# A two-layer trunk on one core: output projection of two heads by seven products of halves, the seven products in another order, part of layer 1's modulation later

## The chip, the cores and the metric

One Trainium2 chip, one core of it. The time is the device time of one execution in microseconds (us). The kernel before took 725.39 us as the median of 3 runs (724.83 to 725.51). The profile that is read here is of one execution of that kernel.

## What is computed

The trunk has two layers over 512 positions of width 1024: layer 0 is a retention mixer with 4 heads (keys 256 wide, values 512 wide), layer 1 a forgetting attention with 16 heads. Each layer is an adaLN-modulated RMS norm, the mixer, and a gated residual add. The part that matters here is layer 0:

```python
shift, scale, gate = jnp.split(c_act @ mod_w[i] + mod_b[i], 3, axis=-1)
h = _rms_norm(x, norm_g[i]) * (1.0 + scale[:, None, :]) + shift[:, None, :]
# _retention(h): w_in gives q, k (rope), values v and a gate path g
q, k, v, g = jnp.split(h @ w_in, [RET_DK, 2 * RET_DK, 2 * RET_DK + RET_DV], axis=-1)
...                                   # chunkwise retention of 4 heads -> o
o = _layer_norm(_from_chunks(o)).reshape(b, s, RET_DV)
y = (o * jax.nn.silu(g)) @ w_out      # w_out is 2048 x 1024: the output projection
x = x + gate[:, None, :] * y          # then layer 1's norm, and layer 1
```

## The kernel before, in words

**Numbers and matmuls.** Every f32 factor of a product is split into a high part (a cast to fp32r on ACT, the tile `wh` for weights) and a low part (the difference, on DVE, `wl`). A product is three matmuls, high by high, high by low and low by high (`mm3`), each 128 x 128 by 128 x 512.

**Order.** Nothing runs in the order of the source. Each instruction is recorded as a task with a priority, and a list scheduler (`Sched.order`) with its own costs lays out one fixed order for each engine. Buffers come from pools by kind: `KINDS` says how many of a kind there may be, and the eight PSUM banks (pool Z) are shared by the kinds `p`, `r`, `s` and `a`. All instructions are issued at one line (L442, in the changed kernel L448), so views of the profile are read by tile names. Each engine takes its instructions strictly in that order, so that an instruction which waits holds everything behind it on its engine. `merge` interleaves a main stretch of work with a side stretch.

**Heads of layer 0.** `head(h)` projects q and k, and then values and gates by `values_gates`: the 512 x 1024 by 1024 x 1024 product is cut into 2 x 2 halves and made by seven products of halves in place of eight (a scheme of Strassen's kind). One product is 24 matmuls of 128 x 512 into two banks. Its weight operand is a block of the weights, a sum of two blocks that DVE adds (`raw<-raw,raw`), or a sum that an accumulating DMA on POOL's queue adds in place (`plus`). Its other operand is a quarter of the transposed input (tiles `act`) or a sum of quarters (tiles `sf`). Banks that hold a partial result and are still needed are copied to `u` on ACT. While head h is projected, the retention of head h-1 runs beside it.

In all heads the products come in this order: first block by quarter (0,0) into banks x; second block by quarter (0,1) into y, then the values of the upper half are put out; sum 1 into v; sum 4 on top of v; sum 2 on top of x, then the gates of the upper half; sum 3 on top of x, then the gates of the lower half (`put_g(1, ...)`, which DVE makes as `big<-u,p`); last quarter (1,1) on top of x. The last product writes the banks that `put_g(1)` reads.

**Output projection.** The gated heads are transposed on the PE (`make_goT`, tiles `go`), the weights are loaded, multiplied by the residual gate on DVE (`raw<-raw,gate`, two of 128 x 512 for a loaded block) and split. `out_a(0)` and `out_a(1)` do heads 0 to 2 for the two halves of the columns into eight accumulators `a`, `out_last` does head 3 tile by tile; `merge(out_a(0), tail3(), ...)` puts head 3's retention beside the first. Then `norm_a(t)` adds the accumulator to x (`x<-a,x`), squares, and rescales (`xn<-x,t`), and `norm_b(t)` transposes (`r<-ident,xn`), modulates and splits into layer 1's input `big`. The first projection of layer 1 is `p<-wh,big`.

**Modulation.** A chunk of shift, scale or gate is a sum over 8 rows of weights on DVE (`macc<-raw,csilu,macc`). Twelve chunks of it (`extra`) are put between the heads' weights.

Of the kernel before, what the change touches and what calls it, by code (L numbers as in the profile page):

```python
# [28 lines left out]
R0, R1, R2 = 0.45, 0.5, 0.84  # L29
# [16 lines left out]
ROPE_AT = 24  # L46

GO = -6.0
# [473 lines left out]
def trunk(tc, x, c, positions, mod_w, mod_b, norm_g, ret_w_in, ret_w_out, fox_w_in, fox_b_f,  # L522
# [6 lines left out]
    with ExitStack() as es:  # L529
# [276 lines left out]
        extra = [its[i:i + 2] for its in extra for i in (0, 2)]  # L806

# [241 lines left out]
        def values_gates(h):  # L1049
# [3 lines left out]
            vc, gc = vcol(h), gcol(h)  # L1053
# [9 lines left out]
            def whole(n):  # L1063
                return [R(("vg", h, n), i) for i in range(2)]

            def plus(raw, col, lo):
                with s.at(SUMS):
                    for i in range(2):
                        G.dma_start(raw[i].rearrange("p (k n) -> p k n", k=2, n=512), rows2(wi0, col, lo + i),
                                    accum_op=ALU.add)  # L1070
                return heads(raw)

# [20 lines left out]
            put_v, put_g = values_out(h), gates_out(h)  # L1093
            x, y, v = [], [], []
            def sum2(raw, other):

                def f(i):
                    V.tensor_tensor(out=raw[i], in0=raw[i], in1=other()[i], op=ALU.add)
                    return heads(raw)(i)
                return f  # L1100

            kept = {}

            def block(n):
                if n not in kept:
                    kept[n] = whole(n)
                return kept[n]
# [563 lines left out]
```

## Time and profile before

| what | value |
|---|---|
| median of 3 runs | 725.39 us (724.83 to 725.51) |
| profiled execution, its own time | 727.05 us |
| span of the profiled execution | 725.3 us |
| PE matmul busy | 706.3 us, 97% of the span |
| DVE busy | 586.7 us, 81% |
| ACT busy | 394.1 us, 54% |
| POOL busy | 118.6 us, 16% |
| mean granted TensorE clock | 0.992 |

The span is the time from the first to the last instruction in the trace; 1.75 us of the execution lie around it. "Busy" of PE comes from matmul records whose ends are modelled and overlap their successors, so the spacing of starts is what a matmul costs. The engine PEld is the loading of the PE's stationary operand.

### The profile page before, as it was taken

What the parts mean: (1) busy time and instruction counts of PE and PEld (TensorE: products, weight loads), DVE (VectorE), ACT (ScalarE), POOL (GpSimd) and SP (SyncE); (2) the same over time, 40 slices, a digit from 0 to 9 for tenths busy, and PEclk for the clock granted to TensorE, in tenths of its full rate; (3) what the DMA queues carried; (4) which work ended last, traced back from release to release, by engine and by line L of the source; (5) the groups of instructions that cost most, each with busy time, mean ns of one, the idle gap of its engine ahead of it and who ended that gap; (6) DMA issues with size and microseconds to landing.
All of it is one profiled execution on the core that took longest, in us unless ns stands there. A gap on an engine that the chain in (4) does not pass through costs nothing.

```text
span 725.3 us, 10079 instructions
## 1 busy us (share of the span) xinstructions
PE 706.3 (97%) x3386; PEld 579.3 (80%) x3386; DVE 586.7 (81%) x1273; ACT 394.1 (54%) x733; POOL 118.6 (16%) x167
## 2 busy tenths in 40 slices
PE   7999999999998999999999999999999999999995
PEld 6777888888887888888888887788887788888884
DVE  5899999989995899899561878887696977789925
ACT  6557574644354426564140553556676577789513
POOL 1001100110100010100000100054343355531011
PEclk9999999999999999999999999999999999999998
DMA  8993773895657755726254317395646565645202
GB/s 288 350 306 81 180 224 105 217 246 173 161 145 174 232 136 151 193 87 204 89 172 145 118 43 249 133 246 142 168 113 155 124 161 138 172 112 186 87 14 103
DMA packets 78547, 118.26 MB, mean 163 GB/s; under 512 B 6952, under 2 KB 39840, under 8 KB 78496
## 3 DMA queue, kind: packets, MB, share of 16 engines
q1 hardware_dynamic: 66176, 98.71, 42.4%
q0 software_dynamic: 12320, 18.91, 14.4%
q8 instruction: 27, 0.44, 0.2%
q14 instruction: 24, 0.20, 0.1%
HBM read 109.16 MB, written 4.25 MB: 156 GB/s over the span
## 4 chain that ended last, share of the span: by engine, by line
PE 82%; DMA 7%; DVE 5%; ACT 3%; issue 2%; POOL 1%; SPq 0%; DVEq 0%; ACTq 0%; POOLq 0%
PE p L442 46%; PE a L442 18%; PE r L442 16%; DMA raw<-in_mod_w 3%; DMA tg<-in_positions 1%; PE s L442 1%; DMA ck<-in_k_mask 1%; DVE macc L442 1%; DVE t L442 1%; POOL lg L442 1%; ACT st L442 1%; DVE st L442 1%; ACT lg L442 1%; ACT wh L442 1%; DMA x<-in_x 1%
## 5 line engine op out<-in xcount | busy, mean ns | idle before, releaser
L442 ACT CAST wh<-raw 128x1024 fp32r<-128x1024 f32 x120 | 124.8, 1052 | 81.4 <-PE p L442 40.5
L442 DVE TENSOR_TENSOR wl<-raw,wh 128x1024 fp32r<-128x1024 f32 x120 | 146.0, 1222 | 26.7 <-ACT wh L442 23.6
L442 PE MATMUL p<-wh,big 128*128 128x512 f32 x384 | 135.7, 402 | 0.0
L442 PEld LDWEIGHTS p<-wh,big 128*128 128x128 f32 x384 | 71.8, 189 | 13.1
L442 PE MATMUL p<-wh,sf 128*128 128x512 f32 x256 | 80.0, 390 | 0.0
L442 PE MATMUL p<-wl,big 128*128 128x512 f32 x192 | 76.5, 398 | 0.0
L442 PE MATMUL p<-wh,act 128*128 128x512 f32 x192 | 64.1, 396 | 1.9 <-DVE big L442 1.9
L442 POOL DMA_DIRECT2D raw<-in_ret_w_in x16 | 19.4, 1240 | 269.6 <-DVE raw L442 88.4
L442 DVE SCALAR_TENSOR_TENSOR macc<-raw,csilu,macc 128x512 f32<-128x512 f32 x80 | 59.8, 747 | 3.5 <-DMA raw<-in_mod_w 2.7
L442 PE MATMUL a<-wh,go 128*128 128x512 f32 x192 | 61.7, 392 | 0.0
L442 PEld LDWEIGHTS p<-wh,sf 128*128 128x128 f32 x256 | 48.0, 188 | 10.8 <-ACT u L442 0.7
L442 POOL TENSOR_SCALAR lg<-lg,t 128x512 f32<-128x512 f32 (+1 forms) x64 | 42.6, 714 | 83.0 <-DVE t L442 68.9
L442 PE MATMUL p<-act,wh 128*128 128x512 f32 x160 | 53.1, 393 | 0.0
L442 PE MATMUL p<-wl,sf 128*128 128x512 f32 x128 | 50.0, 391 | 0.0
L442 PE MATMUL p<-big,wh 128*128 128x512 f32 x128 | 46.3, 419 | 0.0
L442 PEld LDWEIGHTS p<-wh,act 128*128 128x128 f32 x192 | 36.0, 188 | 9.1 <-issue 2.3
L442 PEld LDWEIGHTS a<-wh,go 128*128 128x128 f32 x192 | 36.0, 188 | 7.0
L442 PEld LDWEIGHTS p<-wl,big 128*128 128x128 f32 x192 | 36.2, 189 | 6.2
L442 ACT ACTIVATE lg<-lg,t 128x512 f32<-128x512 f32 (+1 forms) x64 | 35.9, 563 | 9.2 <-DVE t L442 8.7
L442 PE MATMUL r<-act,sh 128*128 128x512 f32 x120 | 40.6, 391 | 0.0
L442 PE MATMUL p<-wl,act 128*128 128x512 f32 x96 | 38.3, 399 | 1.1 <-DVE wl L442 1.1
L442 PE MATMUL a<-wl,go 128*128 128x512 f32 x96 | 37.7, 393 | 0.0
(184 smaller groups left out, 1514.5 us busy)
## 6 DMA issues: line engine op xcount, KB each, us to landing
raw<-in_ret_w_in SPq DMA_DIRECT2D x48, 512.0 KB, 6.1
raw<-in_mod_w SPq DMA_DIRECT2D x64, 256.0 KB, 6.7
raw<-in_fox_w_in SPq DMA_DIRECT2D x32, 512.0 KB, 4.2
raw<-in_ret_w_in POOLq DMA_DIRECT2D x16, 512.0 KB, 8.9
raw<-in_mod_w SPq DMA_DIRECT2D x16, 512.0 KB, 4.6
raw<-in_ret_w_out SPq DMA_DIRECT2D x16, 512.0 KB, 4.3
ck<-cum_dram SPq DMA_DIRECT2D x16, 448.0 KB, 4.4
x<-in_x SPq DMA_DIRECT2D x16, 256.0 KB, 5.3
```

Of the source, the lines that this page charges most:

```text
L442: getattr(eng, op)(*[real(v) for v in args], **{k: real(v) for k, v in kw.items()})
```

## The change

Four things are altered.

1. The output projection of heads 0 and 1 (rows 0 to 1023 of `w_out`) goes by the same seven products of halves: `values_gates` becomes a general `halves`, `make_halves` makes the quarters and sums of the transposed gated heads, and `put_o` puts the results out. Heads 2 and 3 stay with three matmuls per product of tiles into the accumulators `a`.
2. The residual gate is multiplied on the results (`residual`: one multiply `oa<-..,gate`, one add into x) and no longer on the weights. Results of heads 0 and 1 are added into x as they come; those of heads 2 and 3 in `norm_a`. The loads of x stand ahead of the output projection.
3. The seven products come in another order. In all heads sum 2 stands before sum 4, and the last product's accumulating DMA is issued right after sum 2. In heads 1 to 3 (`LAST`) the second product (quarter (0,1) into y) is made late, between sum 3 and the last product.
4. Of the twelve extra chunks of modulation four (`LATE_SS`, layer 1's shift and scale of columns 4 to 7) come between the output weights and not between the heads' weights. Head 0's rope is started at step 32 and not 24; the pool takes six `sx` and four `oa`.

```diff
-R0, R1, R2 = 0.45, 0.5, 0.84
+R0, R1, R2, R3 = 0.45, 0.5, 0.84, 0.35
...
 
-ROPE_AT = 24
-
-GO = -6.0
+ROPE_AT = 32
+
+LATE_SS = 4
+
+GO = (-20.0, -15.0, -10.0, -5.0)
+
+LATER = 4.0
+
+LAST = (1, 2, 3)
...
-            return WItem(wo0[:, 2 * i:2 * i + 2, nh * 512:nh * 512 + 512], 2, 512, (0, nh * 512), place)
+            return WItem(wo0[:, 2 * i:2 * i + 2, nh * 512:nh * 512 + 512], 2, 512, place=place)
...
-            for n in range(4):
+            for i, n in enumerate((0, 2, 3, 1) if h in LAST else range(4)):
                 add(("vg", h, n), its[2 * n:2 * n + 2])
-                if h > 0 and n % 2:
+                if h > 0 and i % 2:
                     spread()
+        its = w_halves(wo0, 0, 512, 0, 2)
+        for n in range(4):
+            add(("oh", n), its[2 * n:2 * n + 2])
         while extra:
             spread()
+        spread2()
         for nh in range(2):
-            add(("o", nh), [w_o(i, nh) for i in range(6)])
+            add(("o", nh), [w_o(i, nh) for i in (4, 5)])
+            spread2()
         for i in (6, 7):
             for nh in range(2):
                 add(("o", nh, i), [w_o(i, nh, lambda k: [act() for _ in range(k)])])
+                spread2()
...
+        def halves(key, src, cols, lows, quarter, sums, put, late=False):
...
             first = block(0)
+
+            def second():
+                yield from product(y, lambda: quarter(0, 1), heads(block(1)), True)
+                put(0, 0, y, u1, ALU.add)
+
             yield from product(x, lambda: quarter(0, 0), heads(first), True)
             u1 = keep(x)
-            yield from product(y, lambda: quarter(0, 1), heads(block(1)), True)
-            put_v(0, y, u1)
-            yield from product(v, lambda: forms[1], sum2(first, lambda: block(2)), True)
-            third = plus(block(2), gc, 2)
+            if not late:
+                yield from second()
+            yield from product(v, lambda: sums[1], sum2(first, 2), True)
+            third = plus(block(2), c1, lo)
             u5 = keep(v)
-            yield from product(v, lambda: forms[4], heads(block(3)), False)
-            yield from product(x, lambda: forms[2], sum2(first, lambda: block(3)), False)
+            yield from product(x, lambda: sums[2], sum2(first, 3), False)
+            fourth = plus(first, c0, lo)
             u2 = keep(x)
-            put_g(0, v, u2)
-            yield from product(x, lambda: forms[3], third, False)
-            put_g(1, u5, x)
-            yield from product(x, lambda: quarter(1, 1), plus(first, vc, 2), False)
-            put_v(1, x, None)
+            yield from product(v, lambda: sums[4], heads(block(3)), False)
+            put(0, 1, v, u2, ALU.subtract)
+            yield from product(x, lambda: sums[3], third, False)
+            put(1, 1, u5, x, ALU.subtract)
+            if late:
+                yield from second()
+            yield from product(x, lambda: quarter(1, 1), fourth, False)
+            put(1, 0, x, None, None)
...
+        def values_gates(h):
+            put_v, put_g = values_out(h), gates_out(h)
+
+            def put(i, j, a, b, op):
+                if j:
+                    put_g(i, a, b)
+                else:
+                    put_v(i, a, b)
+            yield from halves(("vg", h), wi0, (vcol(h), gcol(h)), (0, 2), quarter, forms, put, h in LAST)
...
-            mm3(ps, goT[kt][0][:, ts], goT[kt][1][:, ts], wh, wl, kt == 0, kt == 15)
-
-        with s.at(GO):
-            for h in range(2):
-                run(make_goT(h))
...
-        def out_a(nh):
-            for i in range(6):
-                wh, wl = W(("o", nh), i)
+            mm3(ps, goT[kt][0][:, ts], goT[kt][1][:, ts], wh, wl, kt == 8, kt == 15)
+
+        def gated(t, nh):
+            return gate_t[:, nh * 512:nh * 512 + 512]
+
...
+        def residual(t, nh, y, out=None):
+
+            out = s.buf("oa") if out is None else out
+            V.tensor_tensor(out=out, in0=y, in1=gated(t, nh), op=ALU.mult)
+            V.tensor_tensor(out=x1s[t][nh], in0=out, in1=x1s[t][nh], op=ALU.add)
...
+        def make_halves(b):
+
+            lo, hi = slice(0, 256), slice(256, 512)
+            pss = []
...
+                ps = pr_()
...
+                    last_t[:] = [T.transpose(ps[:, t * P:(t + 1) * P], go[h][t][:, b * P:(b + 1) * P], ident)]
+                yield 0.45
+                pss.append(ps)
...
+            f0, s13, s24 = s.buf("sx"), s.buf("sx"), s.buf("sx")
+            A.copy(f0, pss[0])
+            for key, src, c in (((0, 0), pss[0], lo), ((0, 1), pss[1], lo), ((1, 1), pss[1], hi)):
+                n = 256 if key == (0, 1) else 0
+                if not n:
+                    h, l = s.buf("go", 512, F32R), s.buf("go", 512, F32R)
+                hc, lc = h[:, n:n + 256], l[:, n:n + 256]
+                split(src[:, c], hc, lc)
+                quarters[key][b] = (hc, lc)
+            V.tensor_tensor(out=s13[:, lo], in0=f0[:, hi], in1=pss[1][:, hi], op=ALU.subtract)
+            V.tensor_tensor(out=s13[:, hi], in0=f0[:, lo], in1=f0[:, hi], op=ALU.subtract)
+            V.tensor_tensor(out=s24[:, lo], in0=s13[:, lo], in1=f0[:, lo], op=ALU.subtract)
+            V.tensor_tensor(out=s24[:, hi], in0=pss[1][:, lo], in1=s24[:, lo], op=ALU.add)
+            for src, (n1, n2) in ((s13, (1, 3)), (s24, (2, 4))):
+                h, l = s.buf("go", 512, F32R), s.buf("go", 512, F32R)
+                split(src, h, l)
+                sums[n1][b] = (h[:, lo], l[:, lo])
+                sums[n2][b] = (h[:, hi], l[:, hi])
+
+        def put_o(i, j, a, b, op):
+            with s.at(LATER):
+                for tl in range(2):
+                    if b is None:
+                        residual(2 * i + tl, j, a[tl])
+                    else:
+                        y = s.buf("oa")
...
+                        V.tensor_tensor(out=y, in0=a[tl], in1=b[tl], op=op)
+                        residual(2 * i + tl, j, y, y)
...
+        for b in range(4):
+            with s.at(GO[b]):
+                run(make_halves(b))
...
-        merge(out_a(0), tail3(), 1.0, B0, s)
+        load_x()
+        merge(halves(("oh",), wo0, (0, 512), (0, 2), lambda i, j: quarters[i, j], sums, put_o), tail3(), R3, B0, s)
...
             for nh in range(2):
-                V.tensor_tensor(out=x1[nh], in0=acc[nh, t], in1=x1[nh], op=ALU.add)
+                residual(t, nh, acc[nh, t], xns[t][nh])
...
+        acc = {}
+        with s.after(*last_t):
+            for nh in range(2):
+                for i in range(2):
+                    wh, wl = W(("o", nh), i)
+                    for t in range(NT):
+                        if i == 0:
+                            acc[nh, t] = s.buf("a")
+                        for k in range(2):
+                            out_mm(acc[nh, t], 8 + 2 * i + k, t, wh[k], wl[k])
+        wlast = {(nh, i): W(("o", nh, i)) for i in (6, 7) for nh in range(2)}
```

On the PE, at the end of head 2's seven products: `p_440` and `p_444` are the banks x, `sf4` are sums of quarters (product 6, sum 3), `act` are plain quarters. Before, product 7 follows product 6 on the same banks:

```order
L442 MATMUL p_444_2000<-wh_490_2193,sf4_144_701 128x512
L442 MATMUL p_444_2000<-wh_490_2193,sf4_164_776 128x512
L442 MATMUL p_444_2000<-wl_491_2200,sf4_164_776 128x512
L442 MATMUL p_444_2000<-wh_490_2193,sf4_167_786 128x512
L442 MATMUL p_440_1987<-wh_498_2237,act_99_513 128x512 [waits DVE_49,Activation_49]
L442 MATMUL p_440_1987<-wl_499_2249,act_99_513 128x512
L442 MATMUL p_440_1987<-wh_498_2237,act_104_532 128x512
L442 MATMUL p_440_1987<-wh_498_2237,act_106_537 128x512
L442 MATMUL p_440_1987<-wl_499_2249,act_106_537 128x512
L442 MATMUL p_440_1987<-wh_498_2237,act_108_546 128x512
L442 MATMUL p_444_2000<-wh_498_2237,act_99_513 128x512 [waits DVE_49]
L442 MATMUL p_444_2000<-wl_499_2249,act_99_513 128x512
```

In the changed kernel the banks x are `p_440` and `p_442`. Behind product 6 on the PE comes first the late second product, into `p_487` and `p_490`:

```order
L448 MATMUL p_442_1996<-wh_470_2129,sf4_144_701 128x512
L448 MATMUL p_442_1996<-wh_470_2129,sf4_164_776 128x512
L448 MATMUL p_442_1996<-wl_473_2143,sf4_164_776 128x512
L448 MATMUL p_442_1996<-wh_470_2129,sf4_167_786 128x512
L448 MATMUL p_487_2220<-wh_475_2152,act_99_513 128x512 [waits Activation_49]
L448 MATMUL p_487_2220<-wl_478_2166,act_99_513 128x512 [waits DVE_49]
L448 MATMUL p_487_2220<-wh_475_2152,act_104_532 128x512
L448 MATMUL p_487_2220<-wh_475_2152,act_106_537 128x512
```

and behind its last rows product 7, on the banks x:

```order
L448 MATMUL p_490_2232<-wh_480_2175,act_123_615 128x512
L448 MATMUL p_490_2232<-wh_480_2175,act_124_618 128x512
L448 MATMUL p_490_2232<-wl_482_2186,act_124_618 128x512
L448 MATMUL p_490_2232<-wh_480_2175,act_128_633 128x512
L448 MATMUL p_440_1985<-wh_483_2196,act_99_513 128x512 [waits DVE_49,Activation_49]
L448 MATMUL p_440_1985<-wl_489_2226,act_99_513 128x512 [waits DVE_49]
L448 MATMUL p_440_1985<-wh_483_2196,act_104_532 128x512
L448 MATMUL p_440_1985<-wh_483_2196,act_106_537 128x512
L448 MATMUL p_440_1985<-wl_489_2226,act_106_537 128x512
L448 MATMUL p_440_1985<-wh_483_2196,act_108_546 128x512
L448 MATMUL p_442_1996<-wh_483_2196,act_99_513 128x512 [waits DVE_49]
L448 MATMUL p_442_1996<-wl_489_2226,act_99_513 128x512
```

So 24 matmuls moved between the last write of the banks x by product 6 and the first by product 7, which still waits for DVE.

On DVE, in the output projection: `raw` are loaded weights, `gate_86` the residual gate. Before, in the middle of the stage:

```order
L442 TENSOR_TENSOR raw_761_3393<-raw_761_3393,gate_86 128x512 [waits DMAHW4_49]
L442 TENSOR_TENSOR wl_767_3448<-raw_744_3338,wh_766_3439 128x1024 [waits PE_49,Activation_49]
L442 TENSOR_TENSOR raw_761_3393<-raw_761_3393,gate_86 128x512
L442 TENSOR_TENSOR raw_765_3426<-raw_765_3426,gate_86 128x512 [waits DMAHW5_49]
L442 TENSOR_TENSOR raw_765_3426<-raw_765_3426,gate_86 128x512
L442 TENSOR_TENSOR raw_768_3458<-raw_768_3458,gate_86 128x512 [waits DMAHW6_49,DVE_49]
L442 TENSOR_TENSOR wl_770_3481<-raw_761_3393,wh_769_3473 128x1024 [waits PE_49,Activation_49]
L442 TENSOR_TENSOR raw_768_3458<-raw_768_3458,gate_86 128x512
L442 TENSOR_TENSOR raw_771_3492<-raw_771_3492,gate_86 128x512 [waits DMAHW7_49]
L442 TENSOR_TENSOR wl_774_3514<-raw_765_3426,wh_773_3506 128x1024 [waits PE_49,Activation_49]
L442 TENSOR_TENSOR raw_771_3492<-raw_771_3492,gate_86 128x512
L442 TENSOR_TENSOR raw_777_3527<-raw_777_3527,gate_86 128x512 [waits DMAHW0_49,DVE_49]
```

In the changed kernel, behind the sixth product of the output projection (`p_702`, `p_712` are its banks, `u` copies, `x1` the residual stream, `macc` the modulation that came later):

```order
L448 TENSOR_TENSOR oa_808_3548<-u_759_3321,p_702_3091 128x512 [waits PE_49]
L448 TENSOR_TENSOR go_810_3555<-r_803_3531,go_806_3542 128x512 [waits Activation_49]
L448 TENSOR_TENSOR oa_808_3548<-oa_808_3548,gate_86 128x512 [waits DVE_49]
L448 TENSOR_TENSOR go_812_3567<-r_807_3545,go_811_3558 128x512 [waits Activation_49]
L448 TENSOR_TENSOR x1_632_2846<-oa_808_3548,x1_632_2846 128x512 [waits DMAHW5_49,DVE_49]
L448 TENSOR_SCALAR macc_814_3577<-raw_757_3315,csilu_82 128x512 [waits DMAHW5_49,DMAHW4_49]
L448 TENSOR_TENSOR oa_815_3581<-u_760_3331,p_712_3122 128x512
L448 SCALAR_TENSOR_TENSOR macc_814_3577<-raw_757_3315,csilu_82,macc_814_3577 128x512 [waits DVE_49]
L448 TENSOR_TENSOR wl_821_3597<-raw_772_3391,wh_813_3573 128x1024 [waits DMAHW0_49,DVE_49,Activation_49]
L448 SCALAR_TENSOR_TENSOR macc_814_3577<-raw_758_3318,csilu_82,macc_814_3577 128x512 [waits DMAHW7_49,DMAHW6_49]
L448 TENSOR_TENSOR go_825_3616<-r_809_3553,go_816_3584 128x512 [waits Activation_49]
L448 SCALAR_TENSOR_TENSOR macc_814_3577<-raw_758_3318,csilu_82,macc_814_3577 128x512 [waits DVE_49]
```

The multiplies of weights are gone; in their place stand combinations and multiplies of results, adds into x, and the modulation's sums, among the splits of `go` and of the weights.

On DVE, in layer 1's norm: `xn_829` and `xn_836` are tile 2 rescaled, `a_781` is tile 3's second accumulator. Before:

```order
L442 TENSOR_SCALAR xn_844_3931<-r_840_3916,mod_a_84,mod_s_85 128x128
L442 SCALAR_TENSOR_TENSOR t_842_3923<-t_843_3927,t_842_3923 128x1 [waits DVE_49]
L442 TENSOR_SCALAR xn_844_3931<-r_840_3916,mod_a_84,mod_s_85 128x128
L442 SCALAR_TENSOR_TENSOR t_843_3927<-t_842_3923,t_839_3911 128x1 [waits DVE_49]
L442 SCALAR_TENSOR_TENSOR t_842_3923<-t_843_3927,t_842_3923 128x1 [waits DVE_49]
L442 TENSOR_SCALAR xn_829_3865<-x1_757_3383,t_842_3923 128x512 [waits DVE_49]
L442 TENSOR_SCALAR xn_836_3895<-x1_758_3385,t_842_3923 128x512
L442 TENSOR_TENSOR big_832_3880<-xn_841_3919,big_830_3872 128x4x128 [waits Activation_49]
L442 TENSOR_TENSOR big_837_3903<-xn_844_3931,big_834_3889 128x4x128 [waits Activation_49]
L442 TENSOR_TENSOR x1_760_3390<-a_781_3539,x1_760_3390 128x512 [waits PE_49]
```

In the changed kernel tile 2 rescaled is `xn_889` and `xn_896`, tile 3's accumulators are read by `xn_902` (further up) and `xn_909<-a_851,gate_86`:

```order
L448 TENSOR_TENSOR x1_634_2850<-xn_902_4041,x1_634_2850 128x512
L448 SCALAR_TENSOR_TENSOR t_906_4056<-t_907_4061,t_906_4056 128x1 [waits DVE_49]
L448 TENSOR_TENSOR xn_909_4071<-a_851_3750,gate_86 128x512 [waits PE_49]
L448 SCALAR_TENSOR_TENSOR t_907_4061<-t_906_4056,t_905_4050 128x1 [waits DVE_49]
L448 TENSOR_TENSOR x1_635_2852<-xn_909_4071,x1_635_2852 128x512 [waits DVE_49]
L448 SCALAR_TENSOR_TENSOR t_906_4056<-t_907_4061,t_906_4056 128x1 [waits DVE_49]
L448 SCALAR_TENSOR_TENSOR t_907_4061<-t_906_4056,t_905_4050 128x1 [waits DVE_49]
L448 SCALAR_TENSOR_TENSOR t_906_4056<-t_907_4061,t_906_4056 128x1 [waits DVE_49]
L448 TENSOR_SCALAR xn_889_3966<-x1_631_2844,t_906_4056 128x512 [waits DVE_49]
L448 TENSOR_SCALAR xn_896_4001<-x1_632_2846,t_906_4056 128x512
```

The rescaling of tile 2 moved behind the multiply and the add of tile 3's last accumulator.

## Rows read from the trace of the kernel before

**Rows 1.** Page, busy time of each engine: us, share of the span, instructions.

```profile
PE 706.3 (97%) x3386; PEld 579.3 (80%) x3386; DVE 586.7 (81%) x1273; ACT 394.1 (54%) x733; POOL 118.6 (16%) x167
```

**Rows 2.** PE's waits: line waited for, us in total, times, longest.

```profile
PE p L442 <- DVE big L442: 1.9, 1, 1.9
```

**Rows 3.** Timeline of PE, end of head 2: start, us, instruction [idle before, releaser].

```profile
228.97 0.39 PE L442 MATMUL p<-wh,sf 128*128 128x512 f32 x1
231.28 0.47 PE L442 MATMUL p<-wh,act 128*128 128x512 f32 x1 [1.92 <-DVE big L442]
```

**Rows 4.** Timeline of DVE in the same stretch.

```profile
227.99 0.75 DVE L442 SCALAR_TENSOR_TENSOR macc<-raw,csilu,macc 128x512 f32<-128x512 f32 x1 [2.72 <-DMA raw<-in_mod_w]
228.66 1.22 DVE L442 TENSOR_TENSOR wl<-raw,wh 128x1024 fp32r<-128x1024 f32 x1
229.80 0.74 DVE L442 SCALAR_TENSOR_TENSOR macc<-raw,csilu,macc 128x512 f32<-128x512 f32 x1
230.46 1.28 DVE L442 TENSOR_TENSOR big<-u,p 128x512 f32<-128x512 f32 x2
231.65 0.74 DVE L442 SCALAR_TENSOR_TENSOR macc<-raw,csilu,macc 128x512 f32<-128x512 f32 x1
```

**Rows 5.** Timeline of PE at the end of the output projection.

```profile
393.95 13.77 PE L442 MATMUL a<-act,go 128*128 128x512 f32 x60
407.55 1.03 PE L442 MATMUL r<-ident,xn 128*128 128x128 f32 x8
408.34 0.94 PE L442 MATMUL a<-act,go 128*128 128x512 f32 x3
```

**Rows 6.** Page, costliest groups: matmuls of the output projection, busy and mean ns.

```profile
L442 PE MATMUL a<-wh,go 128*128 128x512 f32 x192 | 61.7, 392 | 0.0
...
L442 PE MATMUL a<-wl,go 128*128 128x512 f32 x96 | 37.7, 393 | 0.0
```

**Rows 7.** Timeline of DVE, operations of 256 columns in head 0.

```profile
52.60 0.42 DVE L442 TENSOR_TENSOR sx<-x,x 128x256 f32<-128x256 f32 x1
52.94 0.42 DVE L442 TENSOR_TENSOR sx<-x 128x256 f32<-128x256 f32 x1
53.27 0.42 DVE L442 TENSOR_TENSOR sx<-sx,x 128x256 f32<-128x256 f32 x1
```

**Rows 8.** Windows of the output stage: us, busy (instructions) of PE, PEld, DVE, ACT, POOL, clock, DMA.

```profile
310.00:335.00 25.00, 25.00 (x131) 21.29 (x129) 22.86 (x63) 13.34 (x28) 0.00 (x0) 1.00 0.45 141
335.00:360.00 25.00, 25.00 (x124) 20.72 (x123) 19.69 (x29) 8.60 (x11) 0.00 (x0) 1.00 0.39 133
360.00:385.00 25.00, 25.00 (x112) 20.71 (x111) 15.07 (x20) 9.63 (x13) 0.00 (x0) 1.00 0.40 130
385.00:410.00 25.00, 25.00 (x116) 20.79 (x115) 8.54 (x29) 4.71 (x13) 2.80 (x5) 1.00 0.45 157
```

**Rows 9.** Timeline of DVE in the norm of layer 1.

```profile
396.87 0.69 DVE L442 TENSOR_TENSOR x<-a,x 128x512 f32<-128x512 f32 x1 [12.54 <-PE a L442]
...
417.00 0.88 DVE L442 TENSOR_SCALAR xn<-x,t 128x512 f32<-128x512 f32 x2
417.79 1.28 DVE L442 TENSOR_TENSOR big<-xn,big 128x512 fp32r<-128x512 f32 x2
419.00 0.68 DVE L442 TENSOR_TENSOR x<-a,x 128x512 f32<-128x512 f32 x1
```

**Rows 10.** Timeline of PE in the norm: last matmuls on `a`, transposes of tile 2.

```profile
414.68 2.98 PE L442 MATMUL a<-act,go 128*128 128x512 f32 x12
...
421.58 1.03 PE L442 MATMUL r<-ident,xn 128*128 128x128 f32 x8
```

**Rows 11.** Groups of DVE by form, 60 to 410 us: busy, mean ns, idle before, releasers.

```profile
L442 DVE TENSOR_TENSOR wl<-raw,wh 128x1024 fp32r<-128x1024 f32 x80 | 97.1, 1221 | 18.6 <-ACT wh L442 16.6 <-issue 1.1
...
L442 DVE TENSOR_TENSOR raw<-raw,gate 128x512 f32<-128x512 f32 x32 | 21.3, 685 | 0.9 <-DMA raw<-in_ret_w_out 0.9
```

**Rows 12.** Page, DMA issues: count, KB each, median us to landing.

```profile
raw<-in_ret_w_in POOLq DMA_DIRECT2D x16, 512.0 KB, 8.9
```

More of the change, by code (lines that the diff above doesn't have):

```diff
@@ L806, in trunk, with spread2 @@
         extra = [its[i:i + 2] for its in extra for i in (0, 2)]
+        extra, extra2 = extra[:12 - LATE_SS], extra[12 - LATE_SS:]
+        def spread2():
+            if extra2:
+                add(("e", len(items)), extra2.pop(0))
         def spread():
@@ L1061, in heads, with block @@
                 return f
-            def whole(n):
-                return [R(("vg", h, n), i) for i in range(2)]
+            kept = {}
+            def block(n):
+                if n not in kept:
+                    kept[n] = [R((*key, n), i) for i in range(2)]
+                return kept[n]
             def plus(raw, col, lo):
@@ L1068, in plus, with sum2, f @@
                     for i in range(2):
-                        G.dma_start(raw[i].rearrange("p (k n) -> p k n", k=2, n=512), rows2(wi0, col, lo + i),
+                        G.dma_start(raw[i].rearrange("p (k n) -> p k n", k=2, n=512), rows2(src, col, lo + i),
                                     accum_op=ALU.add)
                 return heads(raw)
+            def sum2(raw, n):
+                def f(i):
+                    V.tensor_tensor(out=raw[i], in0=raw[i], in1=block(n)[i], op=ALU.add)
+                    return heads(raw)(i)
+                return f
             def product(banks, a, w, new):
@@ L1091, in keep @@
                 return us
-            put_v, put_g = values_out(h), gates_out(h)
             x, y, v = [], [], []
[L1095 to L1107, printed above, removed]
             first = block(0)
+            def second():
+                yield from product(y, lambda: quarter(0, 1), heads(block(1)), True)
+                put(0, 0, y, u1, ALU.add)
@@ L1241, in trunk, with chain @@
             merge(head(h), retention(h - 1), R0, B0, s)
+        def chain(*gens):
+            for g in gens:
+                yield from g
         goT = {}
@@ new lines, in gated, with load_x @@
+        def gated(t, nh):
+            return gate_t[:, nh * 512:nh * 512 + 512]
+        x1s = [[s.buf("x1") for _ in range(2)] for _ in range(NT)]
+        def load_x():
+            with s.at(-20.0):
+                for t in range(NT):
+                    for nh in range(2):
+                        SY.dma_start(x1s[t][nh], xs[t * P:(t + 1) * P, nh * 512:nh * 512 + 512])
+        def residual(t, nh, y, out=None):
+            out = s.buf("oa") if out is None else out
+            V.tensor_tensor(out=out, in0=y, in1=gated(t, nh), op=ALU.mult)
+            V.tensor_tensor(out=x1s[t][nh], in0=out, in1=x1s[t][nh], op=ALU.add)
@@ new lines, in trunk @@
+        quarters, sums = {n: [None] * 4 for n in ((0, 0), (0, 1), (1, 1))}, {n: [None] * 4 for n in (1, 2, 3, 4)}
+        def make_halves(b):
+            lo, hi = slice(0, 256), slice(256, 512)
+            pss = []
+            for h in (0, 1):
+                ps = pr_()
[21 more added lines that the diff above has]
+                sums[n2][b] = (h[:, hi], l[:, hi])
@@ L1577, in proj1 @@
                 yield from proj_b(lambda i: W(("f" + name, g), i), h2, ev, lead=lead)
-        def chain(*gens):
-            for g in gens:
-                yield from g
         q0 = proj1("q", 0, lead=3)
```

33 lines of the change are left out of this document (11 added, 22 removed), and 2 rows, old and new, of the table KINDS.

## The prediction

> **What bounds the kernel now.** I read the page's busy times first, then PE's waits, then the timeline around the one wait that belongs to the change, then the output stage in windows. The reader is to see four things. PE is busy 97% of the span, DVE 81% [rows 1]. PE's longest wait is a single one of 1.9 us for DVE's `big` [rows 2]. In the output projection (310 to 410 us) PE is busy in all of its time, DVE in 22.86 + 19.69 + 15.07 + 8.54 = 66.2 us of 100 [rows 8]. And a matmul of 512 columns costs its start-to-start spacing, not its record's 392 ns [rows 6]: 60 of them start between 393.95 and 407.55, which is 0.227 us each [rows 5]. So the output stage is as long as its matmuls, and one taken away there is worth 0.227 us while DVE, ACT and the loads keep up.
>
> **Matmuls removed.** Heads 0 and 1 have 8 row tiles of weights; with 4 position tiles, 2 column halves and 3 matmuls they took 192 of the 288 matmuls of [rows 6]. Seven products of 24 are 168, so 24 go: 24 x 0.227 = **-5.45 us**. The transposes are as many as before (32).
>
> By [rows 5] the price is thus 5.45 us. The Trainium skill (TensorE: Matmul & The Clock Gate, section Back-to-back issue gap) gives about 131 ns for each 512-column matmul in a sustained stream of weight load and matmul; by it 24 would be worth 3.1 us, 2.3 less. The trace does not agree with it here.
>
> **The wait at the end of head 2.** Product 6 writes banks x, DVE's `big<-u,p` reads them, product 7 writes them again. PE's last matmul of product 6 starts at 228.97, the next at 231.28, idle 1.92 of it [rows 3]: 2.31 - 0.23 = 2.08 us lost. DVE was late there: 2.72 us on a modulation load, then `macc` (0.66), `wl` (1.14), `macc` again, and only at 230.46 `big<-u,p` [rows 4]. Now the late second product stands between, 24 matmuls or 5.45 us, more than the 2.08. What can be late next is that product's weights; by the sums of row durations in the new order they are some 4 us ahead. I take **-2.08 us**; it is 0 if the late product runs into the same late DVE.
>
> **DVE in the output stage.** Unit costs are start-to-start: 128x1024 1.14, 128x512 0.60, `macc` 0.66 [rows 4], 256 columns 0.335 [rows 7], one-source 128x512 0.395 [rows 9]. Gone: 32 multiplies of weights (19.2) and 8 splits of `go` (4.8). New: 6 `wl` (6.8), 4 sums of blocks (4.6), 8 splits of sums (4.8), 28 operations of 256 columns (9.4), 16 gate multiplies (9.6), 6 combinations of banks (3.6), 8 more adds into x (4.8). That is 43.6 - 24.0 = +19.6 us. The late modulation adds 14 x 0.66 + 2 x 0.395 = 10.0, taken out of heads 2 and 3. Three of the gate multiplies (1.8) fall behind 410 us, so DVE has 66.2 + 27.8 = 94.0 us in a stage that would be 94.5 long. It fits only if almost nothing holds DVE up, so I look where it is tightest.
>
> It is behind the fifth product. From the first read of that product's banks (`oa<-p,u`) to the last `macc` of the first late chunk, DVE has 23 operations of 512 columns, 6 `wl`, 7 `macc` and 2 one-source ones: 13.8 + 6.8 + 4.6 + 0.8 = 26.0 us. PE, between the last matmul on that bank and the matmul that takes the chunk's sum (`r<-ones,macc`), has 105 matmuls and 28 transposes. Eight transposes take 0.79 [rows 5], so this is 23.8 + 2.8 = 26.6. Handing over costs about 0.2 each way: `x<-a,x` starts at 396.87 [rows 9], 0.2 behind the start of the matmul after its twelve (393.95 + 12 x 0.227 = 396.67 [rows 5]); PE starts 0.13 after the first of two `big<-u,p` ends (230.46 + 0.69 [rows 3, 4]). So 26.4 against 26.6: a tie. Every wait of DVE for ACT or a load in that stretch is then PE's. DVE waited 16.6 us for ACT in 80 `wl` [rows 11], 0.21 each; six of them are 1.2 us. In addition the late chunks' loads may hold it, 2.72 us in the one case of [rows 4]. Ends: 0 and 3.9. I take **+1.0**, near the casts alone, since the loads are issued well ahead in a stage with DMA shares of 0.39 to 0.45 [rows 8].
>
> The bank wait of head 2 exists here too: product 7 follows product 6 directly. But there DVE has nothing late before it and transposes stand between, 0 to 0.5 us, inside that term.
>
> **Layer 1's norm.** DVE gets eight multiplies, 0.60 each. Before, tile 2 was rescaled at 417.00 to 417.79 and transposed only at 421.58 [rows 9, 10], 3.8 us of slack. The changed order puts the rescale behind the multiply and add of tile 3's last accumulator, which PE finished near 417.4 (414.68 + 12 x 0.227 [rows 10]; its add started at 419.00 only, behind others [rows 9]). Six of the eight multiplies come before it (3.6), and the last accumulator's own two operations (1.2) and handover: it would be ready between 1.2 us before its transposes and 2.4 after. I take **+0.3**, range 0 to 2.4.
>
> **At no cost.** Four more accumulating transfers on POOL's queue: each lands 8.9 us after issue [rows 12]; between the last use of the block by DVE and the product that needs it lie two products (10.9 us) and retention's matmuls. Loads of x move ahead of the output weights on SP's queue; the weights behind them are covered by the same DMA room. Rope at step 32, sum 2 before sum 4: DVE is nearly full in heads 0 and 1, and by the sums five splits there come only 0.2 to 0.8 us ahead of PE. I take 0, with up to 1 us either way. Lighter DVE in heads 2 and 3 gains nothing by itself, as PE waits there only at the place above.
>
> **Sum.** -5.45 - 2.08 + 1.0 + 0.3 = -6.2. The profiled execution took 727.05, 1.66 more than the median of 725.39. So 727.05 - 6.2 = 720.8 on its scale and **719.2 us** on the median's.
>
> **Rivals.**
>
> DVE becomes the bound of the output stage. For it: 94.0 us of work in 94.5, and the tie above. Against it: DVE waits for PE at the fifth product, so what was late before is made good there. Price with both holds: -7.53 + 3.9 + 0.3 = -3.3, or 722.1. The Trainium skill (Perfetto Trace Analysis, section Identifying the Most-Contended Engine) would judge TensorE by its weight loads and DVE by occupancy, and by that DVE (81%) stands a little ahead of PEld (80%) in [rows 1]. The trace agrees over the whole span; in the output stage, with DVE at 66.2 of 100, it does not.
>
> The wait of head 2 stays, since DVE is late at the second product in place of the seventh. For it: the 2.72 us hold of [rows 4] is a load, which the reorder doesn't make earlier. Against: the late product needs only its own `wl`. -5.45 + 1.3 = -4.15, or 721.2.
>
> A matmul taken away gives back less than its spacing (the rule on 131 ns). Against: 60 in a row at 0.227. -3.1 - 2.08 + 1.3 = -3.9, or 721.5.
>
> Slower: in the new products of the output projection the chain DVE sum of blocks, ACT cast, DVE `wl` stands in DVE's queue behind `oa` operations that wait for PE's banks, and each product waits for its weights as product 7 of head 2 did for its bank. Seven times 1.92 is 13.4: -7.53 + 13.4 = +5.9, or 731.3. It decides from four such waits on (7.7), and shows as slower from five. Against it: before the fifth product the sums of rows leave the weights 3 to 10 us of lead.
>
> **How the numbers follow.** Forecast 0.60, DVE as the bound 0.20, the wait stays 0.10, cheap matmuls 0.02, slower 0.08. Without any loss the time is 717.9; runs lie 0.7 apart, so the low end is 717.2. The high end takes in the first three rivals and one more us for the thin leads: 723.2. A measurement here tells 0.2%, 1.45 us, from no change: faster means below 723.9, slower above 726.8. The forecast, the waits and cheap matmuls, and two thirds of the DVE case are faster: 0.60 + 0.10 + 0.02 + 0.14 = 0.86. The rest of the DVE case, with both holds more than once, is within 0.2%: 0.06. Slower 0.08.
>
> **What would show it.** Right: 168 matmuls `p<-..,go` and 96 `a<-..,go` with 96 of head 3; the stretch from head 3's end to the first `r<-ident,xn` some 5 us shorter; no PE wait for `big`; DVE's idle time in the output stage gone, with PE's waits there below 1.5 us, for `macc` or `wl`. Wrong: PE waits for `wl` at several of the seven products, for `big<-u,p` at product 7 of the output or of a head, or for `xn` over 2.4 us; or no shorter spacing of stages although 24 matmuls are gone.

## The result and the profile after

The changed kernel took 719.23 us (median of 4 runs, 719.05 to 720.82) beside 725.45 (724.83 to 725.65) for the kernel before: ratio 0.9921, 95% interval 0.9903 to 0.9938, that is 4.5 to 7.0 us less. A second timing gave 719.39 beside 725.04, again 0.9921 (0.9910 to 0.9933). Forecast was 719.2. The profiled execution took 719.05, with a span of 717.2. Three executions far above all others of their kernel (1132.54, 2924.22 and 780.16 us, of the kernel before and of two experiments below) are left out of every median and ratio here.

The page of the changed kernel, busy times, the weights' splits, and a group that was not there before. Behind an engine's name stand busy us, share of the span and instructions; behind a group, busy us and mean ns:

```profile
PE 700.6 (98%) x3362; PEld 575.1 (80%) x3362; DVE 603.2 (84%) x1309; ACT 409.1 (57%) x761; POOL 123.4 (17%) x171
...
L448 DVE TENSOR_TENSOR wl<-raw,wh 128x1024 fp32r<-128x1024 f32 x126 | 153.4, 1222 | 21.9 <-ACT wh L448 11.3
...
L448 PE MATMUL p<-wh,go 128*128 128x512 f32 x112 | 39.2, 402 | 0.2 <-DVE oa L448 0.2
```

24 matmuls are gone (3386 to 3362), six `wl` have come (120 to 126), and DVE works 16.5 us more by its busy time, where 19.6 had been added up from spacings of starts. Three of PE's waits, columns as in [rows 2], whose wait for `big` no longer appears. The first stands in head 0 and was there before (1.1); the other two are new:

```profile
PE p L448 <- DVE wl L448: 0.6, 1, 0.6
...
PE r L448 <- DVE xn L448: 0.2, 1, 0.2
PE p L448 <- DVE oa L448: 0.2, 1, 0.2
```

The windows that answer to [rows 8]:

```profile
310.00:335.00 25.00, 24.85 (x117) 20.61 (x116) 25.00 (x52) 13.00 (x26) 3.62 (x3) 1.00 0.45 93
335.00:360.00 25.00, 24.84 (x125) 20.24 (x124) 22.83 (x43) 14.99 (x21) 1.21 (x1) 1.00 0.57 161
360.00:385.00 25.00, 25.00 (x115) 20.63 (x114) 24.91 (x40) 9.95 (x14) 0.00 (x0) 1.00 0.77 252
385.00:410.00 25.00, 25.00 (x124) 21.04 (x123) 19.70 (x52) 10.11 (x25) 3.34 (x6) 1.00 0.44 151
```

DVE went from 66.2 to 92.4 us of the hundred and PE is still full: the stage is now filled on both engines.

One sign of the prediction came out smaller. From the last matmul of head 3's projections (L442 before, L448 after) to the first `r<-ident,xn` (407.55 and 399.86) it is 91.05 us in place of 93.44, 2.4 shorter and not some 5:

```profile
314.11 0.39 PE L442 MATMUL p<-wh,act 128*128 128x512 f32 x1
...
308.81 0.39 PE L448 MATMUL p<-wh,act 128*128 128x512 f32 x1
...
399.86 1.03 PE L448 MATMUL r<-ident,xn 128*128 128x128 f32 x8
```

The sums of the late chunks (`r<-ones,macc`, twice eight matmuls, 1.7 us of PE) moved from the heads into this stage, which costs nothing over the whole. PE lost 0.4 at product 7's bank; the 0.9 that is left is taken up again below.

At the end of head 2, PE's timeline in place of [rows 3] has no gap; product 6 ends, the late second product starts 0.23 us behind:

```profile
222.69 0.39 PE L448 MATMUL p<-wh,sf 128*128 128x512 f32 x1
222.92 0.39 PE L448 MATMUL p<-wh,act 128*128 128x512 f32 x1
```

and on DVE, in place of [rows 4], the second `big<-u,p` still comes behind a `macc` and a `wl`, but product 7 now starts only 24 matmuls later:

```profile
221.76 0.69 DVE L448 TENSOR_TENSOR big<-u,p 128x512 f32<-128x512 f32 x1 [0.32 <-PE p L448]
222.37 0.74 DVE L448 SCALAR_TENSOR_TENSOR macc<-raw,csilu,macc 128x512 f32<-128x512 f32 x1
223.20 1.23 DVE L448 TENSOR_TENSOR wl<-raw,wh 128x1024 fp32r<-128x1024 f32 x1
224.34 0.68 DVE L448 TENSOR_TENSOR big<-u,p 128x512 f32<-128x512 f32 x1
```

The hold of 2.72 us for a load is not there any more: the first `big<-u,p` waited for PE alone. Without the second product in between, product 7 would have reached the second bank six matmuls after 222.92, near 224.3, and that bank is read until 225.02; so, by this estimate, 0.7 us is what the 24 matmuls hide here.

### The profile page after: what moved, and what is told of

It reads as the page before. It is cut to its first block, busy times and chain, and to the rows that moved or that the text cites. A ratio compares the mean times of both kernels' runs of the same rounds, so it can differ in the third digit from the quotient of the medians.

```text
span 717.2 us, 10155 instructions
## 1 busy us (share of the span) xinstructions
PE 700.6 (98%) x3362; PEld 575.1 (80%) x3362; DVE 603.2 (84%) x1309; ACT 409.1 (57%) x761; POOL 123.4 (17%) x171
## 4 chain that ended last, share of the span: by engine, by line
PE 78%; DVE 9%; ACT 2%; issue 2%; DMA 1%; POOL 1%; DVEq 0%; POOLq 0%; ACTq 0%
PE p L448 52%; PE r L448 15%; PE a L448 11%; DVE wl L448 1%; DVE t L448 1%; DVE xn L448 1%; POOL lg L448 1%; ACT lg L448 1%; DVE sx L448 1%; DVE st L448 1%; DVE x L448 1%; DVE tg L448 1%; DMA ck<-in_k_mask 1%; DMA st<-st 0%; ACT st L448 0%
## 5 line engine op out<-in xcount | busy, mean ns | idle before, releaser
L448 DVE TENSOR_TENSOR wl<-raw,wh 128x1024 fp32r<-128x1024 f32 x126 | 153.4, 1222 | 21.9 <-ACT wh L448 11.3
L448 ACT CAST wh<-raw 128x1024 fp32r<-128x1024 f32 x126 | 131.3, 1052 | 68.5 <-PE p L448 41.6
L448 PE MATMUL p<-wh,big 128*128 128x512 f32 x384 | 135.6, 402 | 0.0
L448 PEld LDWEIGHTS p<-wh,big 128*128 128x128 f32 x384 | 71.8, 189 | 13.1
L448 PE MATMUL p<-wh,sf 128*128 128x512 f32 x256 | 80.6, 392 | 0.0
L448 PE MATMUL p<-wl,big 128*128 128x512 f32 x192 | 76.4, 398 | 0.0
L448 POOL DMA_DIRECT2D raw<-in_ret_w_in x16 | 19.4, 1212 | 257.1 <-ACT sf L448 62.4
L448 PE MATMUL p<-wh,act 128*128 128x512 f32 x192 | 62.8, 393 | 0.0
L448 DVE SCALAR_TENSOR_TENSOR macc<-raw,csilu,macc 128x512 f32<-128x512 f32 x80 | 59.6, 746 | 0.6
L448 POOL TENSOR_SCALAR lg<-lg,t 128x512 f32<-128x512 f32 (+1 forms) x64 | 42.6, 712 | 82.4 <-DVE t L448 68.2
L448 PEld LDWEIGHTS p<-wh,sf 128*128 128x128 f32 x256 | 48.0, 188 | 9.6
L448 PE MATMUL p<-act,wh 128*128 128x512 f32 x160 | 53.3, 393 | 0.0
L448 PE MATMUL p<-wl,sf 128*128 128x512 f32 x128 | 50.2, 392 | 0.0
L448 PE MATMUL p<-big,wh 128*128 128x512 f32 x128 | 46.4, 420 | 0.0
L448 PE MATMUL r<-act,sh 128*128 128x512 f32 x120 | 42.7, 391 | 0.1
L448 PEld LDWEIGHTS p<-wh,act 128*128 128x128 f32 x192 | 36.0, 188 | 7.3
L448 PEld LDWEIGHTS p<-wl,big 128*128 128x128 f32 x192 | 36.2, 189 | 6.2
L448 ACT ACTIVATE lg<-lg,t 128x512 f32<-128x512 f32 (+1 forms) x64 | 35.9, 562 | 9.1 <-DVE t L448 8.7
L448 PE MATMUL p<-wh,go 128*128 128x512 f32 x112 | 39.2, 402 | 0.2 <-DVE oa L448 0.2
L448 PE MATMUL p<-wl,act 128*128 128x512 f32 x96 | 37.8, 394 | 0.6 <-DVE wl L448 0.6
L448 POOL DMA_DIRECT2D ck<-in_k_mask x32 | 28.5, 1083 | 52.2 <-DVE t L448 52.2
L448 DVE TENSOR_TENSOR ph<-r,ph 128x128 fp32r<-128x128 f32 (+2 forms) x64 | 30.8, 485 | 6.8 <-ACT ph L448 6.3
```

The lines of the kernel that those rows point to most:

```text
L448: getattr(eng, op)(*[real(v) for v in args], **{k: real(v) for k, v in kw.items()})
```

## The experiments

Each was timed against the kernel before on the same chip (its medians there: 724.9 to 725.1).

**The kernel before, profiled again.** No edit.

> The kernel before, unchanged, profiled a second time. Theory: the 1.9 us wait at the end of head 2 hangs on when a modulation load lands (DVE was held 2.72 us for it), so it differs from execution to execution; the wait of this profile lies anywhere from 0 to 2 us, and its span differs from 725.3 by about as much. Rival: the wait belongs to the order and is 1.9 us again, and the 1.66 us that the profiled execution took above the median lie elsewhere. Times equal to the kernel before within 0.3 us either way.

724.94 us, ratio 1.0002 (0.9994 to 1.0011); span 723.1, against 725.3 in the first profile. PE's timeline and DVE's at the end of head 2:

```profile
227.98 0.39 PE L442 MATMUL p<-wh,sf 128*128 128x512 f32 x1
229.47 0.47 PE L442 MATMUL p<-wh,act 128*128 128x512 f32 x1 [1.10 <-DVE big L442]
```

```profile
226.18 0.75 DVE L442 SCALAR_TENSOR_TENSOR macc<-raw,csilu,macc 128x512 f32<-128x512 f32 x1 [1.90 <-DMA raw<-in_mod_w]
```

DVE's hold for the load fell from 2.72 to 1.90, PE's wait from 1.92 to 1.10: 0.82 each. The profile of the next experiment, with the same order in the heads, is a third case: hold 2.63, wait 1.83. The theory holds: the wait follows the lateness of the load. Here PE lost 1.49 - 0.23 = 1.26 us. The wait for `wl` near 68 us, which the expectation of the new order alone (below) takes as the order's, was 0.6 in place of 1.1 without any edit.

**24 matmuls left out of the kernel before.**

```diff
+            if kt in (1, 2, 3):
+                T.matmul(ps, goT[kt][0][:, ts], wh, start=False, stop=False)
+                T.matmul(ps, goT[kt][0][:, ts], wl, start=False, stop=False)
+                return
             mm3(ps, goT[kt][0][:, ts], goT[kt][1][:, ts], wh, wl, kt == 0, kt == 15)
```

> The kernel before without 24 of the 288 matmuls of the output projection of heads 0 to 2: low by high is left out for row tiles 1, 2 and 3 (3 row tiles, 4 position tiles, 2 column halves). All DVE, ACT and load work stays. Theory: start-to-start spacing is the price, 24 x 0.227 = 5.45 us less, 719.9. Rival: a matmul of 512 columns costs 131 ns in a stream and 24 give 3.1 us, 722.3.

719.20 us, ratio 0.9926 (0.9910 to 0.9942): 5.4 us less, 4.2 to 6.5. The spacing's 5.45 lies in it, the rival's 3.1 doesn't. The profiled execution was the slowest of the six, 722.12. In it the wait at the end of head 2 was 1.83 us, and behind it the granted clock fell to half (1.2 GHz): PE's matmuls start 0.42 us apart, up to 234.71, in place of 0.23. The window's last columns are clock, DMA share and GB/s:

```profile
230.79 0.47 PE L442 MATMUL p<-wh,act 128*128 128x512 f32 x1 [1.83 <-DVE big L442]
231.09 0.41 PE L442 MATMUL p<-wl,act 128*128 128x512 f32 x1
231.33 1.03 PE L442 MATMUL p<-wh,act 128*128 128x512 f32 x2
232.15 0.63 PE L442 MATMUL p<-wl,act 128*128 128x512 f32 x1
```

```profile
231.40:234.70 3.30, 3.30 (x9) 2.54 (x8) 2.33 (x3) 3.30 (x5) 0.00 (x0) 0.50 0.00 0
```

Eight starts in 3.4 us where 0.227 each would be 1.8: 1.6 us lost behind the wait. In the first profile of the kernel before, a wait of 1.92 left the clock at full.

**The new order alone**, with the rope at step 24 and at step 32. The edit is the order of `halves` in the change, written into `values_gates`; the second kernel has `ROPE_AT = 32` besides.

> The kernel before with the new order of the seven products alone: sum 2 before sum 4 in all heads, the last accumulating transfer issued behind sum 2, the second product late in heads 1 to 3. The output projection, the gate on the weights, the modulation and the rope stay as before. Theory: no wait for big at the end of head 2 (2.08 us) and the wait for wl at 68 us shorter by about 0.5: some 2.6 us below the first profile of the kernel before, and 1.0 to 2.6 us below it in the medians. Rival: the wait moves to the weights of the late product, and the time is within 0.5 us of the kernel before.

> The new order of the seven products alone, as in reorder_only, with head 0's rope started at step 32; output projection, gate on the weights and modulation as before the change. Theory: the wait for big at head 2's end is gone (1.26 us in the second profile of the kernel before) and the wait for wl at 91 us (0.79 us), which the new order opened, doesn't appear: 1.3 us below the kernel before, no PE wait over 0.3 us between 70 and 310 us. Rival: another wait opens in the heads and the time is that of the kernel before within 0.5 us.

At step 24: 724.30 us, ratio 0.9997 (0.9989 to 1.0006), no measurable gain where 1.0 to 2.6 us were expected. The wait for `big` is gone, but one opens in head 0; PE, and DVE in front of it:

```profile
90.22 0.84 PE L444 MATMUL p<-wh,sf 128*128 128x512 f32 x3
91.69 0.50 PE L444 MATMUL p<-wl,sf 128*128 128x512 f32 x1 [0.63 <-DVE wl L444]
```

```profile
88.61 0.68 DVE L444 TENSOR_TENSOR rt<-rt,trig 128x512 f32<-128x512 f32 x1
89.22 0.68 DVE L444 TENSOR_TENSOR act<-rt,act 128x512 fp32r<-128x512 f32 x1
89.82 0.68 DVE L444 TENSOR_TENSOR rt<-rt,trig 128x512 f32<-128x512 f32 x1
90.42 1.22 DVE L444 TENSOR_TENSOR wl<-raw,wh 128x1024 fp32r<-128x1024 f32 x1
```

The weights' split stands behind the rope's operations. At step 32: 723.09 us, ratio 0.9971 (0.9961 to 0.9981), 1.4 to 2.8 us less, and no PE wait over 0.3 us between 70 and 310. So the order with the later rope is worth some 2 us, a little over the 1.3 expected. The later rope with the old order was not run on the kernel before, so its own share is known only as the difference of these two kernels. The order does more than put a product in between: in all four profiles with the old order in the heads a modulation load held DVE at the end of head 2 (2.7, 1.9, 2.6 and 1.6 us), in none of the eight with the new order. Why the load is no longer late there was not tested.

**The output projection alone, with the old order in the heads.** In `halves`, `LAST = ()`, and for the heads:

```diff
+                yield from product(v, lambda: sums[4], heads(block(3)), False)
+                yield from product(x, lambda: sums[2], sum2(first, 3), False)
+                u2 = keep(x)
...
+                fourth = plus(first, c0, lo)
             yield from product(x, lambda: quarter(1, 1), fourth, False)
```

> The changed kernel with the old order of the seven products in the heads of layer 0 (second product early everywhere, sum 4 before sum 2, the last accumulating transfer issued late); output projection by seven products, gate on the results, late modulation as in the changed kernel. Theory: 24 matmuls fewer are 5.45 us, the waits in the output stage and the norm give back about 0.4, and the wait at the end of head 2 stays: 5.0 us below the kernel before, 720.4. Rival: the modulation taken out of heads 2 and 3 is what frees DVE there, the wait for big is gone without the new order, and the time is that of the changed kernel within 0.5 us.

721.09 us, ratio 0.9948 (0.9935 to 0.9961): 3.8 less, where 5.0 were expected. The rival falls, the wait at head 2 is there; and a second one for `big` has come in head 3, where DVE now works on the sums and splits of the output's operands (`sx`, `go`):

```profile
PE p L448 <- DVE big L448: 1.3, 2, 0.8
```

```profile
229.72 0.47 PE L448 MATMUL p<-wh,act 128*128 128x512 f32 x1 [0.76 <-DVE big L448]
```

```profile
306.41 0.62 PE L448 MATMUL p<-wh,go 128*128 128x512 f32 x2
307.61 0.50 PE L448 MATMUL p<-wh,act 128*128 128x512 f32 x1 [0.58 <-DVE big L448]
```

By the ratios, 3.8 here and 2.1 for the order make 5.9, beside 5.7 for the whole change; the rope stands at 32 in all three kernels.

**Eight more DVE operations, six of them where PE and DVE are level.** At issue, behind each `oa<-..,gate` of heads 0 and 1:

```diff
+                if op == "tensor_tensor" and kw["out"].buf.kind == "oa" and kw["in1"].buf.kind is None:
+                    y = real(kw["out"])
+                    eng.tensor_tensor(out=y, in0=y, in1=y, op=ALU.max)
```

> The changed kernel with one more DVE operation of 128x512 (0.60 us, out = max(out, out), which changes nothing) behind each of the eight multiplies oa<-..,gate of heads 0 and 1; every other instruction keeps its place on its engine. Six of the eight stand between the first read of the fifth product's bank and the last macc of the first late chunk. Theory (DVE and PE are level in that stretch): PE waits 3.6 us more there, up to 4.8 if the two early ones count too; 722.7 to 724. Rival (DVE has room): under 1 us slower, 719.2 to 720.2.

725.58 us, ratio 1.0009 (0.9999 to 1.0019); 6.2 above the changed kernel by the medians, above the 722.7 to 724 expected, and 5.2 by the spans (722.4). From the first `..,go` matmul to the norm's first transposes it is 94.4 us in place of 89.4. In the changed kernel, PE and DVE around the matmul that takes the late chunk's sum:

```profile
373.84 0.39 PE L448 MATMUL a<-wh,go 128*128 128x512 f32 x1
374.16 1.02 PE L448 MATMUL r<-ones,macc 128*128 128x1 f32 x8
```

```profile
373.27 1.41 DVE L448 SCALAR_TENSOR_TENSOR macc<-raw,csilu,macc 128x512 f32<-128x512 f32 x2
```

The first of the two `macc`, the last that is needed, ends at about 374.0; PE starts at 374.16, 0.1 late. With the operations added PE waits, at product 7's bank and at the same sum:

```profile
PE p L448 <- DVE oa L448: 2.0, 1, 2.0
...
PE r L448 <- DVE macc L448: 1.3, 1, 1.3
```

```profile
359.05 0.66 PE L448 MATMUL p<-wh,go 128*128 128x512 f32 x1 [1.97 <-DVE oa L448]
...
378.41 1.41 DVE L448 SCALAR_TENSOR_TENSOR macc<-raw,csilu,macc 128x512 f32<-128x512 f32 x2
```

DVE reaches the `macc` 5.1 us later (378.41 for 373.27), at up to 0.72 us for an added operation with its hand-over, and the sum on PE comes 5.15 later (379.31). So DVE's chain sets the time there: the two are level, and DVE has no room. Behind the wait of 1.97 the clock fell to half here too:

```profile
359.20:362.50 3.30, 3.30 (x9) 2.52 (x10) 3.27 (x7) 0.41 (x1) 0.00 (x0) 0.50 0.44 149
```

In this execution that added nothing, as PE still had 1.3 us to wait at the sum. The 1.0 us by which medians and spans differ is not explained by this trace. A lower granted clock goes with it: the four executions with a mean clock of 0.990 to 0.992, the profiled one among them, took 724.3 to 725.4, the seven with 0.986 or 0.987 took 725.4 to 728.2. Where the clock fell in those, no trace shows.

**All modulation early.** `LATE_SS = 0`.

> The changed kernel with all twelve extra chunks of modulation between the heads' weights, as before the change; 10.0 us of DVE work go back from the output stage to heads 2 and 3. Theory: PE lost only 0.4 us in the output stage and 0.4 in the norm to DVE, so that is the most that can come back; in heads 2 and 3 the fuller DVE costs 0 to 2 us: between 0.8 us faster and 1.5 us slower than the changed kernel. Rival: DVE was the bound of the output stage, and 3 us or more come back.

721.02 us, ratio 0.9948 (0.9936 to 0.9960): 1.6 above the changed kernel by the medians and 2.0 by the ratios, a little past the edge of what I expected; the rival, 3 us faster, falls. PE waits for `wl` at the start of the output stage and again in it:

```profile
312.06 0.39 PE L448 MATMUL p<-wh,go 128*128 128x512 f32 x1
313.22 0.50 PE L448 MATMUL p<-wl,go 128*128 128x512 f32 x1 [0.77 <-DVE wl L448]
```

```profile
361.94 1.09 PE L448 MATMUL a<-wh,go 128*128 128x512 f32 x4
364.32 0.49 PE L448 MATMUL a<-wl,go 128*128 128x512 f32 x1 [1.28 <-DVE wl L448]
```

The first wait shows that DVE, with the modulation in heads 2 and 3, enters the output stage late: from 290 us on it has no marked idle time up to that `wl`. The second doesn't show this: DVE had caught up in between (0.5 us idle for ACT's cast before 340.13), and the `wl` that PE waits for at 364.32 starts at 363.04, though ACT's cast for it had ended at 360.47: `macc`, an add into x and `macc` again stand before it in DVE's order. Another order there was not tried.

**The second product late in the output too.** `put_o, True` in the call of `halves`, and the loads in that order.

> The changed kernel with the second product late in the output projection too, so that product 7 there doesn't follow product 6 on its banks. Theory: the PE wait for oa (0.2 us idle, 0.4 lost) goes, but the six operations that put out the second product's results (3.6 us of DVE) come into the stretch in which DVE and PE are level: 1 to 3 us slower than the changed kernel. Rival: only the bank wait matters, 0.4 us faster.

719.36 us, ratio 0.9923 (0.9911 to 0.9935): as the changed kernel. My 1 to 3 us slower is wrong, and the rival's 0.4 is below what can be told. I had counted DVE's side alone. In this order the stretch from sum 4's bank to the chunk's sum has 141 matmuls and 32 transposes of PE, 35.9 us, against 105 and 28 in the changed kernel; DVE takes 35.4 for its part (340.30 to 375.68), so PE's part grew with it and the sum starts without a wait. The wait for `oa` is gone, a matmul for the second chunk's sum waits 0.27:

```profile
388.85 1.05 PE L448 MATMUL r<-ones,macc 128*128 128x1 f32 x8 [0.27 <-DVE xn L448]
```

**The rope at step 24 in the changed kernel.** `ROPE_AT = 24`.

> The changed kernel with head 0's rope started at step 24, as before the change. Theory: sum 2 before sum 4 needs its weights earlier in head 0, and the rope's DVE work in front of them makes PE wait about 0.8 us for wl near 90 us, as the new order alone did: 720.0. Rival: the rope's place changes nothing, within 0.3 us of the changed kernel.

719.52 us, ratio 0.9925 (0.9913 to 0.9938). The wait is where it was expected:

```profile
92.83 0.50 PE L448 MATMUL p<-wl,sf 128*128 128x512 f32 x1 [0.60 <-DVE wl L448]
```

but neither the 0.8 us expected nor nothing can be told from the time, so that the rope's worth is shown by the pair above (724.30 and 723.09) and not by this one. The wait near 68 us was 1.4 in this profile, against 0.6 in the changed kernel's two.

**The changed kernel again.** No edit.

> The changed kernel, unchanged, profiled and timed a second time beside the kernel before. Theory: 5.45 us for 24 matmuls and 1.26 us for the wait, less 0.4 each for the output stage and the norm: 5.9 us below the kernel before, ratio 0.9919, and the same two small waits at the same places. Rival: the larger difference of the first pair of profiles (8.1 us) is the typical one, ratio 0.989.

719.39 us, ratio 0.9921 (0.9910 to 0.9933); span 717.5, which is 5.6 below the second profile of the kernel before. The same two waits, of 0.16 and 0.21 us, at the same places. So the rival falls: the 8.1 us between the first pair of profiles held 2.2 us that the kernel before lost in that one execution.

## Why the prediction was right, by its steps

- **Matmuls removed, -5.45.** Shown by the kernel with 24 matmuls fewer: 5.4 us. The figure of 131 ns from the Trainium skill (TensorE: Matmul & The Clock Gate, section Back-to-back issue gap) does not hold in this stream.
- **The wait of head 2, -2.08.** The wait is gone, as put. Its size in the kernel before hangs on a load: PE lost 2.08, 1.26 and 2.0 us in three profiles with that order, and the two long ones are of executions above their kernel's median (727.05 for 725.39, 722.12 for 719.20), the short one of an execution at it (724.95 for 724.94). So 1.26 is the likelier price, though the timing of the order with its rope (1.4 to 2.8) fits 2.08 as well. The mechanism was right in part. Product 7 no longer meets a bank that DVE still reads; but the 24 matmuls never had to hide the late load, since the new order did away with the hold itself, which the prediction had as unchanged in its rival.
- **DVE in the output stage, +1.0.** Oversized: PE lost 0.4, at product 7's bank, in the part I had called 0 to 0.5. In the stretch behind the fifth product DVE took 26.5 us (347.46 to 374.0) where 26.0 had been added up, without one marked wait for ACT or a load; I had added 1.0 for such waits. The bank's last matmul started at 346.32, so with the hand-over of 0.2 DVE read it about 0.7 us late; hence it never waited for PE there, and the casts had time. PE took 27.6 (346.55 to 374.16) where 26.6 had been added up, 0.4 of it the wait. So the tie was there, and it cost so little because both sides had been summed too short by about as much (0.5 and 0.6); that is luck. The other 0.6 on PE, part of the 0.9 by which the stage shortened less, is a loss for which the prediction had no term.
- **The norm, +0.3.** PE lost 0.37 at tile 2's transposes, as it was put:

```profile
414.35 0.39 PE L448 MATMUL p<-wh,big 128*128 128x512 f32 x1
414.94 1.09 PE L448 MATMUL r<-ident,xn 128*128 128x128 f32 x8 [0.21 <-DVE xn L448]
```

- **At no cost.** Two points failed in detail. The rope's later step is no free move: without it the new order gains nothing measurable by itself. And "lighter DVE in heads 2 and 3 gains nothing by itself" was wrong: the chunks' later place is worth 1.6 to 2.0 us. The two waits that come back without it are 2.05 us of idle time; DVE's lead at the start of the output stage accounts for 0.77 of them, the rest is the order within the stage.
- **The sum.** -5.45 - 2.08 + 1.3 = -6.2 stands beside -5.45 - 1.26 + 0.8 = -5.9 from the second profile and -5.7 from the ratio. If the wait is 1.26, it was 0.8 too large and the losses 0.5; they cancel in part. The 0.9 that the stage kept has no term in either sum. In the profiles most of it is made up in layer 1 behind the norm, which the change leaves alone: from tile 3's transposes to the end 298.6 to 298.8 us in the two profiles of the kernel before and 297.9 to 298.0 in the changed kernel's, while the kernel with 24 matmuls fewer took 298.0 too. The middle was hit closer than its terms deserved.
- **Rivals.** DVE as the bound of the stage: it is level, and eight more operations, 4.8 us by the sums, cost about 5 by the spans. The changed kernel lies at that edge, on the near side. The wait of head 2 did not move to the late product: no PE wait stands there. The cheaper matmuls fall with the kernel that has 24 fewer. The slower case did not occur: no wait for `wl` at any of the seven products of the output. It is close by, though: with the modulation early PE waits for `wl` twice in that stage.

## What to carry to other kernels

Price a removed matmul by the spacing of starts in its own stage, and check with sums on the next engine, from one bank read to the next operand, whether it can follow; where both sums are equal, further work on that engine alone turned into time (5 us for eight operations), while work that came with matmuls of its own did not. A wait read from one profile may hang on a load: take a second profile of the same kernel before it goes into a sum. And look at the granted clock behind a wait: of three waits of 1.8 to 2.0 us here, two were followed by a stretch at half clock.

## What the runs showed that I had not expected

The same kernel's span differed by 2.2 us between two profiled executions (725.3 and 723.1) at the same granted clock (0.992 and 0.991); 0.82 of it is the one wait at head 2, and 0.56 the wait for `wl` near 68 us (1.13 and 0.57).

The clock fell to half behind two of PE's waits for DVE, of 1.83 and 1.97 us, and did not behind one of 1.92. In the first case that was worth 1.6 us, nearly as much as the wait. Whether it happens in other executions of the kernel before, and so belongs to what the new order saves, is not shown; it would fit an order that is worth 2.1 us where the wait alone is 1.3.
